# Attention scores by row-tiled matmuls instead of zero-padded queries, in an encoder layer on eight cores

## Chip, cores and metric

One Trainium2 chip, all eight NeuronCores; each core works on one of eight sequences with no traffic between cores. The time is that of the slowest core, in device microseconds (us). Executions come in a fast state and sometimes in a slow one, in which cores of one die run longer at a lower granted clock (one execution of the kernel before, in the set of `tile_oldconst`, took 947.07 us: 937.7 to 945.5 us on one die at a mean clock of 0.826 to 0.831, 806.7 to 813.3 on the other at 0.989 to 0.993; in the fast runs of all kernels no core's mean is under 0.978); only fast runs are compared. PE is the tensor engine (PEld its weight loads), ACT the scalar engine, DVE the vector engine. PSUM (`ps` in the records) is the memory into which the matmuls here write, which the planner hands out in banks; copying a result out of it, by ACT or DVE (`kT<-ps`: 0.69 and 0.75 us before), is called an eviction. The MLP is the second half of the layer, with `w_up` and `w_down`.

## The reference, cut to what matters

```python
h = modulate(rms_norm(x, g_mix), sh1, sc1)            # (2048, 1024) a sequence
proj = h @ w_in                                       # [fourier 512 | q 512 | k 512 | v 512]
y_f  = rms_norm(fourier_mix(u_f, w_four), g_four_out)
y_na = rms_norm(neighbourhood_attention(q, k, v, rpb), g_na_out)   # 8 heads of 64, window 8 rows x 16 columns
x = x + gt1 * (concat([y_f, y_na]) @ w_out)
h2 = modulate(rms_norm(x, g_ffn), sh2, sc2)
up = dwconv_centred(h2 @ w_up, conv_w, conv_b)        # width 3
x = x + gt2 * ((silu(up[..., :2816]) * up[..., 2816:]) @ w_down)
return rms_norm(x, g_final)
```

## The kernel before

A kernel is built as a list of operations with their tiles. A planner written in the kernel's own Python places them on the engines before launch: at each step it takes, over all engines, the operation that can start earliest, with durations from small formulas (the "planning constants"), and so fixes each engine's order and the PSUM banks. (Conditioning weights, below, are the matrix `w_ada` that makes the shifts and scales `sh`, `sc` and `gt`.) Change a duration or an operation, and every engine's order can change.

Attention handles 16 query tiles of 128 queries. Two heads of 64 features share a tile of 128 partitions. To keep them apart, queries are stored block-diagonally (`qbd`): for each head a copy in which the other head's 64 rows are zero. Each projection of queries is therefore evicted from PSUM twice, with a 0/0.125 mask as scale. A "unit" is one head pair of one query tile (64 units): four matmuls against four blocks of 128 keys, each with 256 columns (two heads x 128 queries), into two banks; inner tiles have an extra block ("extra scores").

```python
# query eviction, twice: e = 0, 1
for e in range(2):
    EVAC(qbd[:, 4*tb:4*tb+4, j-4, e, :], <PSUM>, 512, ..., scale=hm[:, e:e+1], bias=bqe[:, j-4, e:e+1], tag="q_ev")
# ... cut ...
bs = Bank(2, SB_)                                     # SB_ = banks 0-1 or 2-3
mms([(bs, None)], [(V(bs, c//2, (c%2)*256, (c%2+1)*256), kT[:, hp, (jb+c)*128:(jb+c+1)*128],
                    qbd[:, i, hp, :, :], True, True) for c in range(4)], "qk")
ACT(pf, <both banks>, AF.Exp, 1024, ...)              # then x exp(bias) on DVE, then the value product
# ... cut: planning constants ...
def act_ns(n, psum, ptr=0, accum=False): return n / 1.2 + 110 + 85 * ptr + (200 if accum else 0)
def dve_ns(n, mode=1.0):                 return n / (0.96 * mode) + 130
DMA_RATE = 290.0; DMA_LAT = 1900.0
```

The rest of the mixer stage (input projection, Fourier transform, output projection, second norm) is planned into the same stretch of time as attention; the MLP comes after it.

The softmax here doesn't subtract the row's maximum and nothing guards it: scores larger than these inputs give would overflow.

## Time and profile before

| | before |
|---|---|
| median of the first three runs | 814.93 us (814.04 to 815.93) |
| spans of the cores, profiled run | 804.1 to 814.7 us |
| mixer stretch: first projection matmul to first matmul of the MLP | 282.7 us mean of eight cores, 279.5 us on core 4 |
| matmuls of the MLP and after (core 4) | 323.2 to 796.3 us, not touched by the change |

Lines of the page of the slowest core (core 1): its span, the busy time of each engine with its share, and the chain of work that ended last, by engine.

```profile
span 814.7 us, 11668 instructions; the slowest of 8 cores (804.1 to 814.7 us)
...
PE 750.1 (92%) x4781; PEld 381.3 (47%) x4781; DVE 553.7 (68%) x752; ACT 449.8 (55%) x695; POOL 50.0 (6%) x91
...
PE 76%; DMA 11%; ACT 7%; DVE 4%; issue 1%; SPq 0%; POOL 0%; POOLq 0%
```

The chain is mostly PE; but most of that is the MLP.

The table of windows of core 4: for each window busy us of the engines (instructions), granted PE clock, DMA share, GB/s.

```profile
core 4: us, PE busy (x) PEld busy (x) DVE busy (x) ACT busy (x) POOL busy (x), PEclk, DMA share, GB/s
...
140.00:200.00 60.00, 55.08 (x593) 33.79 (x592) 43.54 (x86) 46.64 (x82) 3.70 (x7) 1.00 0.76 185
...
260.00:300.00 40.00, 38.47 (x348) 23.09 (x347) 32.99 (x73) 38.75 (x93) 2.14 (x4) 1.00 0.73 208
...
sum 305.00, PE 287.78 PEld 166.59 DVE 211.47 ACT 254.34 POOL 17.70; mean PE 47.96 PEld 27.77 DVE 35.24 ACT 42.39 POOL 2.95
```

From 140 to 200 us and from 260 to 300 us nothing is idle for long: PE 92% to 96%, ACT 78% to 97%, DVE 73% to 82%, DMA about three quarters.

What touches the query tile on core 4: count, shortest/median/longest in ns, first and last start in us.

```profile
L694 PE MATMUL ps<-qbd,kT x304: 219/272/283, 63.7 to 286.1; 128*128 128x256 bf16 x128, 128*128 128x128 bf16 x24
L761 ACT ACTIVATE qbd<-ps,bqe,colp_s x19: 761/777/801, 62.9 to 216.4; 128x512 bf16<-128x512 f32 x19
L766 DVE TENSOR_SCALAR qbd<-ps,colp_s,bqe x13: 800/807/811, 61.8 to 175.7; 128x512 bf16<-128x512 f32 x13
```

304 score matmuls (256 of them 256 columns wide; the counts after the semicolon, here x128 and x24, are of a sample, here every second matmul) and 32 evictions, 19 x 0.777 + 13 x 0.807 = 25 us of ACT and DVE.

The timeline of PE around one unit (start, us, what):

```profile
121.42 0.60 PE L694 MATMUL ps<-qbd,kT 128*128 128x256 bf16 x4
121.86 0.29 PE L694 MATMUL ps<-Vx,pT_80 128*128 128x65 bf16 x4
```

The four score matmuls start at 121.42 and the next group at 121.86: 0.44 us a unit.

The first starts of the input projection and of the MLP's up projection on core 4 (two views of tiles, one line each; after the shortest, median and longest duration stand the first and the last start):

```profile
L694 PE MATMUL ps<-hT_64,win x192: 376/379/634, 43.7 to 192.4; 128*128 128x512 bf16 x192
```

### The profile page before, as it was taken

The numbers are of one execution on the slowest core, as the hardware profiler recorded it, in microseconds if no ns is written. First come the engines' busy times: TensorE is split into PE (matmuls) and PEld (weight loads), VectorE is DVE, ScalarE is ACT, GpSimd is POOL, SyncE is SP. The second block draws the span as 40 slices with busy tenths as digits, with TensorE's granted clock in tenths as the row PEclk, the third lists the DMA queues.
The fourth block names the chain that finished last, engine by engine and source line by source line (L and its number), as shares of the span: only waits on it lengthen the run. The fifth ranks groups of instructions, "written<-read, shape, count | busy, mean of one in ns | idle before, by whom it ended". The sixth has DMA issues, their size and how long they took to land.

```text
span 814.7 us, 11668 instructions; the slowest of 8 cores (804.1 to 814.7 us)
## 1 busy us (share of the span) xinstructions
PE 750.1 (92%) x4781; PEld 381.3 (47%) x4781; DVE 553.7 (68%) x752; ACT 449.8 (55%) x695; POOL 50.0 (6%) x91
## 2 busy tenths in 40 slices
PE   1269999889999899989999999999999999999996
PEld 1134566456465555544444444444444454444442
DVE  2348596468577785459898989898988954443343
ACT  4468897678679898764545454545454503111112
POOL 0000000010000000122000000000000110000000
PEclk9999999989999999999999999999999999999999
DMA  8899763995311559999222222222223472232321
GB/s 229 292 293 304 231 125 69 189 185 166 100 54 35 185 137 286 238 161 162 39 39 40 38 36 35 37 40 38 39 39 40 40 142 104 103 130 104 125 83 77
DMA packets 38613, 97.87 MB, mean 120 GB/s; under 512 B 11808, under 2 KB 12192, under 8 KB 37536
## 3 DMA queue, kind: packets, MB, share of 16 engines
q1 hardware_dynamic: 18864, 71.30, 26.4%
q0 software_dynamic: 19696, 25.83, 22.8%
q8 instruction: 37, 0.61, 0.3%
q14 instruction: 16, 0.13, 0.1%
HBM read 106.16 MB, written 16.78 MB: 151 GB/s over the span
## 4 chain that ended last, share of the span: by engine, by line
PE 76%; DMA 11%; ACT 7%; DVE 4%; issue 1%; SPq 0%; POOL 0%; POOLq 0%
PE ps L694 75%; DMA mst_100<-w_ada 2%; DMA mst_98<-w_ada 1%; PE ps L699 1%; DMA mst_99<-w_ada 1%; DMA xs_129<-x 1%; DMA stb_127<-w_ada 1%; DMA stb_125<-w_ada 1%; DMA stb_128<-w_ada 1%; DMA xr_135<-x 1%; DMA stg_122<-w_in 1%; ACT pT_80 L719 1%; ACT pT_81 L719 1%; DMA xs_131<-w_out 1%; ACT pT_79 L719 1%
## 5 line engine op out<-in xcount | busy, mean ns | idle before, releaser
L694 PE MATMUL ps<-wd,aT 128*128 128x512 bf16 x704 | 152.4, 379 | 0.0
L731 DVE SCALAR_TENSOR_TENSOR accv<-ps,colp_s,accv 128x1023 f32<-128x1023 f32 (+1 forms) x88 | 112.6, 1280 | 33.4 <-ACT accv L719 32.5
L731 DVE SCALAR_TENSOR_TENSOR accg<-ps,colp_s,accg 128x1023 f32<-128x1023 f32 (+1 forms) x88 | 112.7, 1280 | 7.9 <-ACT accg L719 6.4
L694 PEld LDWEIGHTS ps<-wd,aT 128*128 128x128 bf16 x704 | 68.7, 98 | 82.4
L719 ACT ACTIVATE accg<-ps,colp_s 128x1024 f32<-128x1024 f32 x44 | 53.0, 1206 | 96.4 <-PE ps L694 96.4
L719 ACT ACTIVATE sgm<-accg 128x1024 bf16<-128x1024 f32 x44 | 46.5, 1057 | 44.5 <-DVE accg L731 44.4
L694 PE MATMUL ps<-hT_61,wup_86 128*128 128x512 bf16 x256 | 56.9, 379 | 1.9 <-ACT hT_61 L761 1.9
L719 ACT ACTIVATE accv<-ps,colp_s 128x1024 f32<-128x1024 f32 x44 | 52.6, 1195 | 9.1 <-PE ps L694 9.1
L694 PE MATMUL ps<-hT_61,wup_87 128*128 128x512 bf16 x256 | 56.6, 379 | 0.0
L725 DVE TENSOR_TENSOR aT<-sgm,accv 128x1024 bf16<-128x1024 bf16 x44 | 53.5, 1216 | 0.0
L694 PE MATMUL ps<-hT_64,win 128*128 128x512 bf16 x192 | 48.6, 401 | 2.0 <-DVE win L725 2.0
L694 PE MATMUL ps<-hT_61,wup_89 128*128 128x512 bf16 x224 | 49.5, 379 | 0.0
L694 PE MATMUL ps<-hT_61,wup_91 128*128 128x512 bf16 x224 | 49.5, 379 | 0.0
L694 PE MATMUL ps<-hT_61,wup_88 128*128 128x512 bf16 x224 | 49.5, 379 | 0.0
L694 PE MATMUL ps<-hT_61,wup_90 128*128 128x512 bf16 x224 | 49.5, 379 | 0.0
L694 PE MATMUL ps<-hT_65,win 128*128 128x512 bf16 x192 | 43.9, 379 | 0.0
L725 DVE TENSOR_TENSOR td_153<-ps,gt_140 128x512 f32<-128x512 f32 x16 | 11.1, 691 | 45.6 <-PE ps L694 45.6
L694 PE MATMUL ps<-qbd,kT 128*128 128x256 bf16 (+1 forms) x304 | 41.3, 274 | 0.5 <-ACT pT_80 L719 0.3
L694 PEld LDWEIGHTS ps<-hT_61,wup_86 128*128 128x128 bf16 x256 | 24.9, 98 | 31.8 <-ACT hT_61 L761 2.1
L694 PEld LDWEIGHTS ps<-hT_61,wup_87 128*128 128x128 bf16 x256 | 25.0, 98 | 30.2
L694 PE MATMUL ps<-wo,yna 128*128 128x512 bf16 x128 | 33.5, 384 | 1.6 <-DVE yfT L763 0.8
L694 PEld LDWEIGHTS ps<-hT_61,wup_88 128*128 128x128 bf16 x224 | 21.9, 98 | 26.4
(364 smaller groups left out, 1141.7 us busy)
## 6 DMA issues: line engine op xcount, KB each, us to landing
wd<-w_down POOLq DMA_DIRECT2D x22, 256.0 KB, 6.2
xs_129<-x SPq DMA_DIRECT2D x6, 512.0 KB, 7.3
mst_98<-w_ada SPq DMA_DIRECT2D x3, 1024.0 KB, 7.2
mst_99<-w_ada SPq DMA_DIRECT2D x3, 1024.0 KB, 6.9
xs_130<-x SPq DMA_DIRECT2D x5, 512.0 KB, 6.7
xs_131<-x SPq DMA_DIRECT2D x5, 512.0 KB, 6.9
mst_100<-w_ada SPq DMA_DIRECT2D x2, 1024.0 KB, 6.7
stg_121<-w_in SPq DMA_DIRECT2D x4, 512.0 KB, 5.7
```

The source lines that it names most:

```text
L694: return [e.matmul(of(), lhsT=l, rhs=r, start=s0, stop=s1) for of, l, r, s0, s1 in items]
L699: return [e.transpose(out=of(), in_=i, identity=ident) for of, i in items]
L719: return P.add("act", lambda e: e.activation(out=out, in_=(in_() if callable(in_) else in_), func=func, **kw), act_ns(n, callable(in_), pt ...
L725: return P.add(eng, lambda e: e.tensor_tensor(out=out, in0=in0() if callable(in0) else in0, in1=in1() if callable(in1) else in1, op=op), d ...
L731: return P.add("dve", lambda e: e.scalar_tensor_tensor(out=out, in0=in0() if callable(in0) else in0, scalar=s, in1=in1() if callable(in1) ...
```

## The change

Intent: store queries once (`qT`, scaled by 0.125), and let two 64-row matmuls, one a head, run side by side in the upper and lower half of the array, each into its own bank. That removes the multiplications by zero and half of the query evictions. The planner gets a duration of 320 ns for the eight matmuls of a unit (it had counted 437 ns for four), new formulas, meant to be more exact, for ACT and DVE, other DMA constants, and the conditioning weights get a fourth staging buffer. The diff, cut to its core:

```diff
-DMA_RATE = 290.0
-DMA_LAT = 1900.0
+DMA_RATE = 270.0
+DMA_LAT = 2300.0
-    return n / 1.2 + 110 + 85 * ptr + (200 if accum else 0)
+    return n / 1.2 + (50 if psum else 93) + 93 * ptr + (93 if accum else 0)
-def dve_ns(n, mode=1.0):
-    return n / (0.96 * mode) + 130
+def dve_ns(n, mode=1.0, ptr=0):
+    return n / (0.96 * mode) + 65 + 61 * ptr
 ... (callers pass ptr; tables and tiles re-laid out; masks removed) ...
-        mst = [... for i, o_ in enumerate((R3, R3 + 8 * K, R2))]
+        mst = [... for i, o_ in enumerate((R3, R3 + 8 * K, Q0 + 32 * K, Q0 + 40 * K))]
-                for e in range(2):
-                    EVAC(qbd[:, 4 * tb:4 * tb + 4, j - 4, e, :], ..., scale=hm[:, e:e + 1], bias=bqe[:, j - 4, e:e + 1], tag="q_ev")
+                EVAC(qT[:, 4 * tb:4 * tb + 4, j - 4, :], ..., scale=0.125, bias=bc_, tag="q_ev")
-                bx = Bank(1, FB_)          # extra scores: 4 matmuls of 128 columns, one exponential of 512
+                bx = Bank(2, [4, 5, 6])    # 8 matmuls of 64 rows x 64 columns, two exponentials of 256, dur=280.0
-                    mms([(bs, None)], [(... V(bs_, c // 2, (c % 2) * 256, (c % 2 + 1) * 256)), kT[:, hp, ...],
-                                        qbd[:, i, hp, :, :], True, True) for c in range(4)], "qk")
+                    mms([(bs, None)], [(... V(bs, e, c * 128, (c + 1) * 128)), kT[e * 64:(e + 1) * 64, hp, ...],
+                                        qT[e * 64:(e + 1) * 64, i, hp, :], True, True)
+                                       for c in range(4) for e in range(2)], "qk", dur=320.0)
```

More of the change, by code (lines that the diff above doesn't have):

```diff
@@ L478, in _layout_inputs @@
     g = np.where(valid[None], g, f32(-1e30))
-    ua = g[:, :16].reshape(4, 2, 8, 2, 128, 64).transpose(4, 0, 2, 1, 3, 5).reshape(128, 4 * 8 * 2 * 2 * 64)
-    ux = g[:, 17].transpose(1, 0, 2).reshape(128, 512)
+    ua = g[:, :16].reshape(4, 2, 8, 2, 128, 64).transpose(4, 0, 1, 2, 3, 5).reshape(128, 4 * 8 * 2 * 2 * 64)
+    ux = g[:, 17].reshape(4, 2, 128, 64).transpose(2, 1, 0, 3).reshape(128, 512)
     utab = np.zeros((9, 128, 1024), f32)
@@ L496, in _layout_inputs @@
            np.asarray(inp["conv_w"][0], f32).reshape(3, 44, 128).transpose(2, 0, 1).reshape(128, 132),
-           col(inp["conv_b"][0], 44), 0.125 * (np.arange(128)[:, None] // 64 == np.arange(2)[None, :]).astype(f32)], axis=1)
+           col(inp["conv_b"][0], 44)], axis=1)
     shared = dict(_CONST)
@@ L539, in build_nc @@
     w_down = din("w_down", [DFF, D])
-    colp_d = din("colp", [128, 234])
+    colp_d = din("colp", [128, 232])
     utab_d = din("utab", [9, 128, 1024])
@@ L571, in build_nc @@
         ctab = small("ctab_s", [128, 514], BF16)
-        colp = small("colp_s", [128, 234], F32)
+        colp = small("colp_s", [128, 232], F32)
         ccs = small("ccs", [128, 8], F32)
@@ L581, in build_nc @@
         bcol = small("bcol", [128, 12], F32)
-        bqe = small("bqe", [128, 4, 2], F32)
         ss = small("ss", [128, 5, 16], F32)
@@ L599, in build_nc @@
         cb = colp[:, 188:232]
-        hm = colp[:, 232:234]
         R0 = 3200
@@ L616, in build_nc @@
         R2 = R1 + 16 * K
-        pT = [T(f"pT{i}", R2 + i * 2 * K, [128, 4, 2, 2, 64], BF16) for i in range(3)]
-        pX = [T(f"pX{i}", R2 + 6 * K + i * 2 * K, [128, 4, 2, 2, 64], BF16) for i in range(2)]
+        pT = [T(f"pT{i}", R2 + i * 2 * K, [128, 2, 4, 128], BF16) for i in range(3)]
+        pX = [T(f"pX{i}", R2 + 6 * K + i * 2 * K, [128, 2, 4, 2, 64], BF16) for i in range(2)]
         peX = [T(f"peX{i}", R2 + 10 * K + i * K, [128, 512], BF16) for i in range(2)]
@@ L625, in build_nc @@
         R3 = R2 + 16 * K
-        U = T("U", R3, [128, 4, 8, 256], BF16)
+        U = T("U", R3, [128, 4, 2, 8, 128], BF16)
         UX = T("UX", R3 + 16 * K, [128, 512], BF16)
-        mst = [T(f"mst{i}", o_, [128, 8, 256], F32) for i, o_ in enumerate((R3, R3 + 8 * K, R2))]
         Q0 = R3 + 17 * K
-        qbd = T("qbd", Q0, [128, NT, 4, 2, 128], BF16)
-        yna = T("yna", Q0, [128, NT, 8, 128], BF16)
+        mst = [T(f"mst{i}", o_, [128, 8, 256], F32) for i, o_ in enumerate((R3, R3 + 8 * K, Q0 + 32 * K, Q0 + 40 * K))]
+        qT = T("qT", Q0, [128, NT, 4, 128], BF16)
+        yna = T("yna", Q0, [128, NT, 4, 128], BF16)
         kT = T("kT", Q0 + 32 * K, [128, 4, S], BF16)
@@ L732, in STT @@
                                                                  in1=in1() if callable(in1) else in1, op0=op0, op1=op1),
-                         dve_ns(n), reads=rd, writes=[out], banks=banks, tag=tag)
+                         dve_ns(n, 1.0, 0 if isinstance(s, float) else 1), reads=rd, writes=[out], banks=banks, tag=tag)
         def TS(out, in0, s1, op0, n, mode=1.0, s2=None, op1=None, banks=(), tag="ts"):
@@ L742, in fn @@
                 return e.tensor_scalar(out=out, in0=in0() if callable(in0) else in0, **kw)
-            return P.add("dve", fn, dve_ns(n, mode), reads=rd, writes=[out], banks=banks, tag=tag)
+            return P.add("dve", fn, dve_ns(n, mode, sum(not isinstance(v, float) for v in (s1, s2) if v is not None)), reads=rd, writes=[out],
+                         banks=banks, tag=tag)
         def EVAC(out, in_, n, banks, mode=1.0, scale=None, bias=None, tag="evac", engs=("act", "dve")):
@@ L766, in fn @@
                 return e.tensor_scalar(out=out, in0=src, scalar1=scale, scalar2=bias, op0=ALU.mult, op1=ALU.add)
-            op = P.add(engs, fn, {"act": act_ns(n, True, ptr), "dve": dve_ns(n, mode)}, reads=rd, writes=[out], banks=banks, tag=tag)
+            op = P.add(engs, fn, {"act": act_ns(n, True, ptr), "dve": dve_ns(n, mode, ptr)}, reads=rd, writes=[out], banks=banks, tag=tag)
             return op
@@ L785, in fn @@
                 return e.tensor_scalar(out=out, in0=in_, scalar1=r_, scalar2=None, op0=ALU.mult)
-            op = P.add(("dve", "act"), fn, {"act": act_ns(n, False, 1), "dve": dve_ns(n, 2.0) + 80}, reads=[in_, r_], writes=[out], tag=tag)
+            op = P.add(("dve", "act"), fn, {"act": act_ns(n, False, 1), "dve": dve_ns(n, 2.0, 1)}, reads=[in_, r_], writes=[out], tag=tag)
             return op
@@ L799, in build_nc @@
         load("sp", ctab, ctab_d, "c1", 131072)
-        load("sp", colp, colp_d, "c2", 119808)
+        load("sp", colp, colp_d, "c2", 118784)
         MEMSET("dve", epsb, EPS, 1)
@@ L839, in mod_load32 @@
             nmw[0] += 1
-            st_ = mst[n % 3]
+            st_ = mst[n % 4]
             k = next_stg()
-            load("sp", st_, w_ada[blk, q], f"mst{n % 3}", 1048576, tag="wada")
+            load("sp", st_, w_ada[blk, q], f"mst{n % 4}", 1048576, tag="wada")
             CP("act", stb[k][:, 0:4, :], st_[:, 0:4, :], 1024, tag="wada_cast")
@@ L910, in bias_col @@
             mms([(b, None)], [((lambda: V(b, 0, 0, 1)), r3[:, kc, :], sh1[:, kc:kc + 1], kc == 0, kc == 7) for kc in range(8)], "bias")
-            if 4 <= j < 8:
-                TS(bqe[:, j - 4, :], hm, lambda: V(b, 0, 0, 1), ALU.mult, 2, banks=[(b, None)], tag="bias_fin")
-            else:
-                CP("dve", bcol[:, j:j + 1], lambda: V(b, 0, 0, 1), 1, banks=[(b, None)], tag="bias_fin")
+            TS(bcol[:, j:j + 1], lambda: V(b, 0, 0, 1), 0.125 if 4 <= j < 8 else 1.0, ALU.mult, 1, banks=[(b, None)], tag="bias_fin")
         def fm_group(tb, j):
@@ L930, in fm_evac @@
             elif j < 8:
-                for e in range(2):
-                    EVAC(qbd[:, 4 * tb:4 * tb + 4, j - 4, e, :], lambda: V(b, 0, 0, 512).rearrange("p (t q) -> p t q", t=4), 512,
-                         [(b, None)], scale=hm[:, e:e + 1], bias=bqe[:, j - 4, e:e + 1], tag="q_ev")
+                EVAC(qT[:, 4 * tb:4 * tb + 4, j - 4, :], lambda: V(b, 0, 0, 512).rearrange("p (t q) -> p t q", t=4), 512,
+                     [(b, None)], scale=0.125, bias=bc_, tag="q_ev")
             else:
@@ L976, in build_nc @@
                 load("sp", stg[k], utab_d[k9], f"stg{k}", 524288, tag="utab")
-                ACT(U[:, k9 // 2, 4 * (k9 % 2):4 * (k9 % 2) + 4, :].rearrange("p m n -> p (m n)"), stg[k], AF.Exp, 1024, tag="utab_exp")
+                ACT(U[:, k9 // 2, k9 % 2, :, :].rearrange("p m n -> p (m n)"), stg[k], AF.Exp, 1024, tag="utab_exp")
             else:
@@ L996, in attn_tile @@
             if inner:
-                bx = Bank(1, FB_)
+                bx = Bank(2, [4, 5, 6])
                 px = pX[i % 2]
                 pex = peX[i % 2]
-                mms([(bx, None)], [((lambda hp=hp: V(bx, 0, hp * 128, (hp + 1) * 128)), kT[:, hp, (jb + 4) * 128:(jb + 5) * 128],
-                                    qbd[:, i, hp, :, 64:128], True, True) for hp in range(4)], "qkx")
-                ACT(pex, lambda: V(bx, 0, 0, 512), AF.Exp, 512, banks=[(bx, None)], tag="expx")
-                TT("dve", px.rearrange("p h e a q -> p (h e) a q")[:, :, 1, :], pex.rearrange("p (g q) -> p g q", g=8),
+                mms([(bx, None)],
+                    [((lambda hp=hp, e=e: V(bx, e, hp * 64, (hp + 1) * 64)), kT[e * 64:(e + 1) * 64, hp, (jb + 4) * 128:(jb + 5) * 128],
+                      qT[e * 64:(e + 1) * 64, i, hp, 64:128], True, True) for hp in range(4) for e in range(2)], "qkx", dur=280.0)
+                for e in range(2):
+                    ACT(pex[:, e * 256:(e + 1) * 256], lambda e=e: V(bx, e, 0, 256), AF.Exp, 256, banks=[(bx, e)], tag="expx")
+                TT("dve", px.rearrange("p e h a q -> p (e h) a q")[:, :, 1, :], pex.rearrange("p (g q) -> p g q", g=8),
                    UX.rearrange("p (g q) -> p g q", g=8), ALU.mult, 512, mode=2.0, tag="mulx")
@@ L1011, in attn_tile @@
                     bs = Bank(2, SB_)
-                    mms([(bs, None)], [((lambda c=c: V(bs_, c // 2, (c % 2) * 256, (c % 2 + 1) * 256)), kT[:, hp, (jb + c) * 128:(jb + c + 1) * 128],
-                                        qbd[:, i, hp, :, :], True, True) for bs_ in (bs,) for c in range(4)], "qk")
-                    pf = pt.rearrange("p c e a q -> p (c e a q)")
+                    mms([(bs, None)], [((lambda c=c, e=e, bs=bs: V(bs, e, c * 128, (c + 1) * 128)),
+                                        kT[e * 64:(e + 1) * 64, hp, (jb + c) * 128:(jb + c + 1) * 128], qT[e * 64:(e + 1) * 64, i, hp, :], True, True)
+                                       for c in range(4) for e in range(2)], "qk", dur=320.0)
+                    pf = pt.rearrange("p e c n -> p (e c n)")
                     ACT(pf, (lambda bs=bs: ps[:, bs.phys:bs.phys + 2, :].rearrange("p b n -> p (b n)")), AF.Exp, 1024,
@@ L1027, in attn_tile @@
                     for c0, c1, sl in parts:
-                        w = pf[:, c0 * 256:c1 * 256]
-                        TT("dve", w, w, U[:, hp, sl:sl + c1 - c0, :].rearrange("p m n -> p (m n)"), ALU.mult, (c1 - c0) * 256, mode=2.0,
+                        w = pt[:, :, c0:c1, :].rearrange("p e c n -> p e (c n)")
+                        TT("dve", w, w, U[:, hp, :, sl:sl + c1 - c0, :].rearrange("p e m n -> p e (m n)"), ALU.mult, (c1 - c0) * 256, mode=2.0,
                            tag="mul")
@@ L1035, in attn_tile @@
                         for c in range(4):
-                            items.append((of, pt[:, c, e, :, :], Vx[:, jb + c, h, :], c == 0, c == 3 and not inner))
+                            items.append((of, pt[:, e, c, :], Vx[:, jb + c, h, :], c == 0, c == 3 and not inner))
                         if inner:
-                            items.append((of, px[:, hp, e, :, :], Vx[:, jb + 4, h, :], False, True))
+                            items.append((of, px[:, e, hp, :, :], Vx[:, jb + 4, h, :], False, True))
                     mms([(bo, None)], items, "pv")
@@ L1052, in attn_tile @@
             trs([(bt, None)], [((lambda c=c: Vb(bt)[:, c * 128:(c + 1) * 128]), ob[:, c * 128:(c + 1) * 128]) for c in range(4)], "tro")
-            EVAC(yna[:, i, 0:4, :].rearrange("p c t -> p (c t)"), lambda: Vb(bt)[:, 0:512], 512, [(bt, None)], mode=2.0, tag="yna_ev")
+            EVAC(yna[:, i, :, :].rearrange("p c t -> p (c t)"), lambda: Vb(bt)[:, 0:512], 512, [(bt, None)], mode=2.0, tag="yna_ev")
         def inproj(tb, part):
```

## The prediction

> **What bounds the kernel now.** The chain of waits puts 76% on the tensor engine (PE), 11% on DMA, 7% on ACT, 4% on DVE. From about 353 us on (gated MLP, down projection) the chain is one unbroken run of matmuls, 454 us long, which the change does not touch. The change can act only on the first 353 us. There the table of windows shows three regimes: 0 to about 65 us, DMA (share 0.85 to 1.0 in most windows, PE nearly idle); 65 to 297 us, where attention, input projection, Fourier and output projection are interleaved, with PE busy about 95%, ACT about 80%, DVE about 70%; and 297 to 353 us, output projection and second norm. The chain in the middle stage is mostly PE, with ACT stretches at 92-112, 246-256 and 288-296 us, and DMA (conditioning weights) at 135-175 us.
>
> **What changes, costed.**
> 1. Score matmuls. Before: 64 units of 4 matmuls with 256 columns, half of them multiplied by zeros. In the timeline eight start within 0.87 us, 109 ns each, so 435 ns a unit, 28 us in all; the extra-block scores take 48 x 56 ns = 2.7 us. After: 8 matmuls of 64 rows and 128 columns a unit. If two run side by side at the 56 ns at which 128-column transposes start here, a unit would take 224 ns; but every matmul also needs its own weight load, and the closest pace shown is 31 ns for a matmul with its load (value products, 65 columns), so at least about 250 ns. The diff plans 320 ns (and 280 ns for the extra block, against 4 x 56). [...] Saving: 64 x 115 ns = 7.4 us, minus 12 x 57 ns = 0.7 us: 6.7 us of PE.
> 2. Query evictions: 32 (19 on ACT at 0.78 us, 13 on DVE at 0.81 us: 25 us) become 16 with one pointer less, about 0.7 us: 14 us less over two engines, before 225 us.
> 3. The extra exponential splits in two: [...] it also takes two adjacent banks of a pool of four.
> 4. A fourth staging buffer in the DMA-bound opening: 1 to 2 us at most, because the bytes remain.
> 5. New planning constants: every engine's order is replanned. Gain or loss of some us, not computable from the trace.
>
> **On the critical path.** Of item 1 some 70-80% (PE is the limit of most of the middle stage, but also waits on ACT and DMA there): 5 us. Of item 2 the part in ACT-bound stretches: 2 to 3 us. Item 4: 1 us. Item 5: 1 us gain expected, uncertain by 4. Sum about -9.5 us: 805.5 us, range 797 to 812.
>
> **What would show it.** Score matmuls: 512 + 96 in place of 304, a unit starting within about 0.32 us (right) or over 0.43 us (wrong); query evictions x16; MLP run again about 454 us long, starting at 341 to 347 us instead of 353; ACT stretches near 92-112 us shorter; first input-projection matmul 0 to 2 us earlier than 45.5 us.
>
> **What would make it wrong.** [...] a stage that turns out bound by ACT exponentials (64 x 0.91 us) or by conditioning-weight DMA, so that PE savings become idle time; the replanned order moving transfers into each other; a better plan than I credit, gaining over 16 us.

The sum is 5 (item 1) + 2.5 (item 2) + 1 (item 4) + 1 (item 5) = 9.5 us; the 320 ns of item 1 are the diff's plan. The 70-80% of item 1, the 2 to 3 us of item 2, item 4 and item 5 are estimates of mine, with no measured number behind them. What the trace of before shows for the rest: as many weight loads as matmuls on PE (4781 each); starts 56 ns apart for 128 columns and 29 to 30 ns for the value products (the record has 31); evictions with one pointer less, those of `kT`, at 0.69 us on ACT and 0.75 on DVE; exponentials of 1024 columns at 1.02 us whole, of which 0.91 us stands in the chain.

## More of the kernel before

```profile
L694 PE MATMUL ps<-hT_61,wup_86 x256: 379/379/389, 323.2 to 633.9; 128*128 128x512 bf16 x128
```

323.2 - 43.7 = 279.5 us of mixer stretch.

## The result, and the profile after

812.5 us median of four runs (811.68 to 813.85) against 815.43 us of before's four, one of them slow. The ratio of fast runs is 0.9971, with a 95% interval of 0.9949 to 0.9993: about 2.4 us faster, where I had said 9.5, and just above the range of 797 to 812 us. (Ratios here are the mean time of one kernel's fast runs over the mean of the other's fast runs of the same rounds, so they are not quite ratios of the medians quoted.) Run again on another chip it gave 0.9977.

The page of the slowest core after (core 6):

```profile
span 810.9 us, 12199 instructions; the slowest of 8 cores (803.2 to 810.9 us)
...
PE 736.2 (91%) x4999; PEld 369.6 (46%) x5085; DVE 549.5 (68%) x746; ACT 447.4 (55%) x697; POOL 49.2 (6%) x91
...
PE 75%; ACT 12%; DMA 8%; DVE 2%; issue 1%; SPq 0%; POOLq 0%
```

ACT's share of the chain has risen from 7% to 12%, while the PE share is as before. The MLP hides how large this is. Within the mixer stretch alone, as a mean of the eight cores, PE held 53% of the chain before (ACT 22%, DMA 15%, DVE 8%) and 53% after (ACT 35%, DMA 6%, DVE 4%). On the slowest cores, ACT's part of the chain between 255 and 300 us grew from 10.5 to 34.6 us. The windows of core 4 after:

```profile
core 4: us, PE busy (x) PEld busy (x) DVE busy (x) ACT busy (x) POOL busy (x), PEclk, DMA share, GB/s
...
140.00:200.00 60.00, 56.52 (x706) 33.66 (x705) 40.69 (x83) 48.34 (x87) 4.14 (x8) 1.00 0.77 179
...
260.00:300.00 40.00, 36.78 (x374) 20.53 (x369) 30.17 (x68) 39.08 (x89) 2.88 (x6) 1.00 0.80 230
...
sum 305.00, PE 282.84 PEld 156.05 DVE 204.99 ACT 251.22 POOL 16.66; mean PE 47.14 PEld 26.01 DVE 34.16 ACT 41.87 POOL 2.78
```

In the sum line PE's busy time fell by 5 us, ACT's by 3 and DVE's by 6.5; in the window from 260 to 300 us ACT is busy 98% and PE 92% (before: 97% and 96%).

The query tile after, on core 4:

```profile
L692 PE MATMUL ps<-qT,kT x608: 189/216/227, 67.8 to 284.5; 64*128 64x128 bf16 x128, 64*128 64x64 bf16 x24
L765 DVE TENSOR_SCALAR qT<-ps,bcol x9: 745/751/752, 65.5 to 166.6; 128x512 bf16<-128x512 f32 x9
L760 ACT ACTIVATE qT<-ps,bcol x7: 672/687/687, 68.0 to 216.3; 128x512 bf16<-128x512 f32 x7
```

608 score matmuls of 64 rows and 16 evictions of 0.69 or 0.75 us: as planned, 11.6 us in place of 25.

The timeline of PE on core 4 after:

```profile
108.06 0.62 PE L692 MATMUL ps<-qT,kT 64*128 64x128 bf16 x16
108.61 1.90 PE L692 MATMUL ps<-winv,hT_64 128*128 128x512 bf16 x8
...
111.26 0.29 PE L692 MATMUL ps<-Vx,pT_80 128*128 128x65 bf16 x4
111.38 0.20 PE L692 MATMUL ps<-Vx,pX_81 128*128 128x65 bf16 x1
111.51 0.40 PE L692 MATMUL ps<-qT,kT 64*128 64x128 bf16 x8
111.84 0.39 PE L692 MATMUL ps<-winv,hT_64 128*128 128x512 bf16 x1
```

Read three things. Two units in a row (16 matmuls) take 108.61 - 108.06 = 0.55 us. One unit alone takes 111.84 - 111.51 = 0.33 us until the next full-array matmul starts. And the last value product ahead of it starts at 111.38; the next matmul could have started 29 ns later, at 111.41, but the tiled one starts at 111.51. From the single records over the whole trace: the two halves of a pair start 3 to 4 ns apart, the next pair 53 ns later, so four pairs stream in 226 ns; but going from full-array to tiled costs 96 ns over the usual distance (for instance 312 in place of 216 ns after a 512-column matmul), and going back costs 95 ns (148 in place of 53). Each such step, in or out, is called a switch below; here it costs about 95 ns. What happens in the array during it the trace does not show.

So a unit alone costs 226 + 191 = 417 ns, hardly less than the 436 ns of before (436 / 226 = 1.9 without the switches, 436 / 417 = 1.05 with them); two in a row cost 321 ns each, which is the 320 ns of the plan. Of the 51 groups in which the plan issued tiled matmuls, 31 hold only eight. Adding up all score matmuls: 30.6 us before; 15.8 us of streaming plus 102 switches for 9.7 us after. PE work fell by 5.1 us.

The trace of before already held a delay of this size, and I overlooked it when I made the prediction. There, two groups of matmuls have weights with a single column (`128*1`). On every core the step into them takes 309 or 310 ns where 216 is usual, and the step out 152 in place of 56 or 312 in place of 216, so 93 to 96 ns each way. That these delays have the same cause as the switches was not tested. The first group, on core 4 of before:

```profile
216.72 0.59 PE L694 MATMUL ps<-winv,hT_65 128*128 128x512 bf16 x2
217.24 0.38 PE L694 MATMUL ps<-AB,ue_58 128*1 128x128 bf16 x4
217.56 0.34 PE L694 MATMUL ps<-AB,uT 128*128 128x128 bf16 x3
```

The ends of the stretch on core 4 after:

```profile
L692 PE MATMUL ps<-hT_63,win x192: 376/379/634, 46.9 to 194.3; 128*128 128x512 bf16 x192
```

```profile
L692 PE MATMUL ps<-hT_60,wup_85 x256: 379/379/390, 326.7 to 637.3; 128*128 128x512 bf16 x128
```

326.7 - 46.9 = 279.8 us, against 279.5 before, on two cores whose clock never dropped in it. Taking for every core the usual distance between starts for the form of each matmul (216 ns for 512 columns, 109 for 256, 56 for 128, 29 for 65, 25 for one), and calling the rest pauses, I get for core 4 (a half-clock spell is a time in which the granted clock is 0.50, and what it costs counts as pause too): before 254.1 us of work and 25.4 of pauses, after 239.3 + 9.7 us of work and 30.8 of pauses. The 5 us of PE work came back as 5 us of pauses. Over all eight cores the stretch is 282.7 us before, 281.0 after.

On undisturbed cores nothing was gained (280.1 us before, mean of three; 279.9 after, mean of four); the 1.7 us over all cores come with fewer spells of half clock. On core 1 before, PE waited for conditioning weights:

```profile
174.67 0.59 PE L694 MATMUL ps<-cs,stb_127 128*128 128x1 bf16 x16 [2.96 <-DMA stb_127<-w_ada]
```

and the windows of core 1 around it show what followed (columns as above):

```profile
170.00:173.80 3.80, 1.56 (x25) 0.96 (x21) 3.00 (x7) 2.60 (x3) 0.00 (x0) 1.00 1.00 199
173.80:180.60 6.80, 5.93 (x68) 4.72 (x69) 2.74 (x8) 3.72 (x7) 1.06 (x2) 0.50 0.90 196
```

PE was 41% busy for 3.8 us, and then the granted clock was 0.50 for 6.8 us. The 15 spells in the stretch (before and after together) last 3.4 us, two of them 6.8. In the 3.4 us before this one PE was busy for a third of the time, with no pause over 2.2 us, and in the 3.4 us before each of the 15 it was busy for 26 to 64%, with no pause over 2.3 us. What brings a spell on is not shown beyond that. Before, five of the eight cores had such a spell in the stretch, up to 10.2 us a core; after, four had, up to 6.8 us. On core 1 the pause was a wait for a transfer (2.96 us, above); how many cores have spells varies from run to run (five had one when the changed kernel ran again).

What happened to ACT's share of the saved evictions: over the whole program ACT's instructions sum to 491.3 us on before's slowest core and 487.4 us on after's, 4 us less, though query evictions fell there by 10.0 us. The splitting of the extra exponential took 1.9 us (24 x 0.384 in place of 12 x 0.609), and the new plan put 5 more of the wide norm scalings (1.15 us on ACT, 0.75 on DVE) and 3 more transposed-input evictions (1.02 against 0.69) on ACT, and fewer of other evictions.

### The profile page after: what moved, and what is told of

Its sections match the earlier page's. It is cut to its first block, busy times and chain, and to the rows that moved or that the text cites. A ratio compares the mean times of both kernels' runs of the same rounds, so it can differ in the third digit from the quotient of the medians.

```text
span 810.9 us, 12199 instructions; the slowest of 8 cores (803.2 to 810.9 us)
## 1 busy us (share of the span) xinstructions
PE 736.2 (91%) x4999; PEld 369.6 (46%) x5085; DVE 549.5 (68%) x746; ACT 447.4 (55%) x697; POOL 49.2 (6%) x91
## 4 chain that ended last, share of the span: by engine, by line
PE 75%; ACT 12%; DMA 8%; DVE 2%; issue 1%; SPq 0%; POOLq 0%
PE ps L692 74%; DMA xs_130<-x 2%; ACT pT_80 L717 1%; ACT rstd L717 1%; DMA stb_127<-w_ada 1%; ACT pT_79 L717 1%; ACT pT_78 L717 1%; DMA wf<-w_four 1%; DMA mst_97<-w_ada 1%; DMA mst_100<-w_ada 1%; PE ps L697 1%; DMA mst_99<-w_ada 1%; DMA stg_121<-w_in 1%; DMA mst_98<-w_ada 1%; ACT hT_60 L760 1%
## 5 line engine op out<-in xcount | busy, mean ns | idle before, releaser
L692 PE MATMUL ps<-hT_63,win 128*128 128x512 bf16 x180 | 44.5, 389 | 9.0 <-DVE sh_51 L723 3.7
L692 PE MATMUL ps<-hT_64,win 128*128 128x512 bf16 x184 | 42.7, 379 | 0.8 <-issue 0.6
L723 DVE TENSOR_TENSOR td_153<-ps,gt_140 128x512 f32<-128x512 f32 x16 | 11.1, 691 | 44.9 <-PE ps L692 44.9
L692 PEld LDWEIGHTS ps<-hT_60,wup_85 128*128 128x128 bf16 x256 | 24.9, 98 | 31.7 <-ACT hT_60 L760 2.0
L692 PEld LDWEIGHTS ps<-hT_60,wup_86 128*128 128x128 bf16 x256 | 25.1, 98 | 30.2
L692 PEld LDWEIGHTS ps<-hT_60,wup_90 128*128 128x128 bf16 x224 | 21.9, 98 | 26.4
L692 PEld LDWEIGHTS ps<-hT_60,wup_88 128*128 128x128 bf16 x224 | 21.9, 98 | 26.4
L692 PEld LDWEIGHTS ps<-hT_60,wup_87 128*128 128x128 bf16 x224 | 21.9, 98 | 26.4
```

The source lines that it names most:

```text
L692: return [e.matmul(of(), lhsT=l, rhs=r, start=s0, stop=s1) for of, l, r, s0, s1 in items]
L723: return P.add(eng, lambda e: e.tensor_tensor(out=out, in0=in0() if callable(in0) else in0, in1=in1() if callable(in1) else in1, op=op), d ...
```

## The experiments

Two theories at the start. **A**: the stretch is bound by PE, tiling did save 5 us, and an unlucky new order gave them back. **B**: PE had stopped being what decides there; other engines and transfers decide, so less PE work turns into pauses. All ratios are to the kernel before in the same rounds, five rounds each; the changed kernel stands at 0.9971 and 0.9977. I give differences to the changed kernel as differences of these ratios times 815 us. The runs were made in four sets of four, each set on one chip: `tile_oldconst`, `pad_newconst`, `score_twice`, `more_switches`; `after_again`, `u_half`, `q_ev_twice`, `pair_units`; `act_light`, `both_light`, `norm_on_dve`, `pair_norm_dve`; and the last four below. Only the second set has the changed kernel itself beside it, so differences in the other sets go through before, on another chip. Each ratio has a 95% interval of about +-0.002 to 0.003, so a difference of two of them is uncertain by 2 to 3 us, and a worth of PE time below by about 0.2 (`pair_switches`: 0.4).

**1. Which part of the change?** `tile_oldconst`: the changed kernel with before's planning constants.

```diff
-    return n / 1.2 + (50 if psum else 93) + 93 * ptr + (93 if accum else 0)
+    return n / 1.2 + 110 + 85 * ptr + (200 if accum else 0)
# likewise dve_ns, DMA_RATE, DMA_LAT
```

> The changed kernel planned with the planning constants of before (tiled matmuls, single query eviction, four staging buffers kept). Theory A (the tiling saves about 5 us of PE after its switches, and the new plan gives it back as waits): 3 to 6 us faster than the changed kernel, about 806 to 809 us, ratio to before 0.990 to 0.994. Rival B (the middle stage is bound by ACT, DVE and DMA, so less PE work turns into idle time under any plan): as the changed kernel, 811 to 814 us.

Measured: 817.15 us median, ratio 0.9986 (0.9964 to 1.0008). Theory A's 0.990 to 0.994 fails here: with the old constants the tiled kernel is not shown to be faster than before. PE work is 239.6 + 11.2 us (59 groups), pauses 33.5 us.

`pad_newconst`: the kernel before with the new constants.

> The kernel before (padded queries, two evictions) with only the planning constants changed. Theory A: the new constants cost 3 to 6 us, so 818 to 821 us, and PE slack between the first projection matmul and the first up matmul grows by about 5 us. Rival B: the constants alone do nothing, 813 to 817 us.

Measured: 818.68 us, ratio 1.0027 (1.0004 to 1.0049), about 2 us slower. On its four undisturbed cores the stretch is 285.4 us where before's three have 280.1: as theory A had it and theory B did not, though the slowest core shows only half of that. (Before's slowest core spent 10.2 us of the stretch at half clock; in this kernel's profile one core had one half-clock spell, of 3.4 us.) The two together make a square (ratios; padded/old is 1):

| | old constants | new constants |
|---|---|---|
| padded, two evictions | 1 | 1.0027 |
| tiled, one eviction | 0.9986 | 0.9971, 0.9977 |

The same tiling (with the single eviction) is worth 1 us under one plan and 4 under the other, and the constants cost 2 us on the padded kernel and gain 1 on the tiled one. Apart from the 4 us none of these is well clear of its uncertainty, so this square suggests, and does not show, that the parts do not add; `pair_oldconst` below shows it.

**2. What is PE time worth there?** The order on every engine stays fixed in these runs; only instructions within an operation change, and the planner is not told. `score_twice` issues every pair twice.

```diff
+  its = [it for k in range(0, len(items), 2) for it in items[k:k + 2] * 2] if tag == "qk" else items
```

> The changed kernel, same order on every engine, every pair of score matmuls issued twice (same result): 64 x 226 ns = 14.5 us more PE work in tiled mode, no switch more. Theory A (PE bound there): 10 to 14.5 us slower than the changed kernel, 822 to 827 us. Rival B: the waits absorb most, under 6 us slower.

Measured: 819.14 us, ratio 1.0028 (1.0009 to 1.0047): about 4.4 us slower for 14.1 us more PE work, so 0.3 us for each. Pauses fell to 25.3 us. Theory B.

`more_switches` puts one full-array column in the middle of each unit.

```diff
+  mid=(V(bs, 1, 384, 385), kT[:, hp, jb*128:(jb+1)*128], qT[:, i, hp, 0:1], True, True)
+  its = items if mid is None else items[:4] + [mid] + items[4:]
```

> The changed kernel, same order, one full-array matmul of one column in the middle of each of the 64 units (its column is overwritten afterwards, same result): two more mode switches a unit. If a switch costs 95 ns each way as the trace of the change suggests, 64 x (2 x 95 + 25) = 13.8 us more PE time; theory A: 9 to 14 us slower than the changed kernel. If the 95 ns were an artefact of the records (waits on banks or on data), each unit would grow by 25 to 60 ns only and the time by under 4 us.

Measured: 821.85 us, ratio 1.0057 (1.0027 to 1.0086), about 6.8 us slower for 13.1 us more, so 0.5 for each. The cost of a switch is confirmed in the timeline. The same two units with the extra scores, on core 6 of the changed kernel:

```profile
101.44 0.74 PE L692 MATMUL ps<-qT,kT 64*128 64x128 bf16 x24
102.11 1.90 PE L692 MATMUL ps<-winv,hT_64 128*128 128x512 bf16 x7
```

and on core 3 of this one:

```profile
102.30 1.17 PE L693 MATMUL ps<-qT,kT 64*128 64x128 bf16 x26
103.40 0.82 PE L693 MATMUL ps<-winv,hT 128*128 128x512 bf16 x3
```

102.11 - 101.44 = 0.67 us against 103.40 - 102.30 = 1.10 us: 0.43 us for two inserted columns, 215 ns each, of which a single column without switches takes 25 ns (from start to start in the traces of before and after). The 60 ns in the expectation was an estimate of mine.

`u_half` is the opposite: it leaves out half of the contraction of the Fourier channels' projection (wrong result).

```diff
+  its = items[:3] + items[7:] if tag == "u_half" else items
```

`after_again` is the changed kernel as control on that chip.

> The changed kernel itself, as control on this chip for the three others. Ratio to before 0.995 to 0.999.

> The changed kernel, same order, with 4 of the 8 contraction chunks of the Fourier channels' projection left out (wrong result on purpose): 64 x 216 ns = 13.8 us less PE work, all of it within the middle stage, nothing else touched. Theory A (the stage is PE-bound and the 5 us saved by tiling were lost to an unlucky order): 8 to 13 us faster than the changed kernel, about 800 to 805 us. Rival B (PE has stopped being the limit there, other engines and transfers decide): under 4 us faster, PE slack in the stretch grows by about 10 us or more.

Measured: 0.9977 (0.9958 to 0.9995) for the control, 0.9935 (0.9905 to 0.9964) for `u_half`: 3.4 us faster for 13.8 us less PE work, so a quarter of it. (The two intervals touch, and one of the six fast executions, 814.88 us, lies 6 us above the next; without it the gain would be 4.6 us, a third.) The first starts of the two projections on core 1, control first, neither core with a half-clock spell:

```profile
L692 PE MATMUL ps<-hT,win x384: 376/379/634, 46.7 to 217.0; 128*128 128x512 bf16 x192
```

```profile
L692 PE MATMUL ps<-hT,wup x1408: 379/379/390, 327.8 to 645.3; 128*128 128x512 bf16 x176
```

```profile
L693 PE MATMUL ps<-hT,win x320: 376/379/631, 44.9 to 210.3; 128*128 128x512 bf16 x160
```

```profile
L693 PE MATMUL ps<-hT,wup x1408: 379/379/390, 321.2 to 638.6; 128*128 128x512 bf16 x176
```

327.8 - 46.7 = 281.1 and 321.2 - 44.9 = 276.3 us. PE work fell from 249.2 to 235.4 us and pauses grew from 32.8 to 43.1 us (means of the cores with complete records). This run and `score_twice` decide for B as to what PE time is worth: most of the PE work taken away or added went into pauses or came out of them.

Half-clock spells blur these numbers: the profile of `score_twice` has none in the stretch, that of the control has at least one on five cores. On the cores without any drop of the clock in it, the stretch is 279.9 us in both profiles of the changed kernel, 287.3 in `score_twice` (four cores), 286.2 in `more_switches` (two) and 277.1 in `u_half` (two): 0.5 for each microsecond added and 0.2 for each taken away. All of this is the worth in the order of the changed kernel; in the order of before it was not measured.

**3. What decides instead?** `q_ev_twice` makes each query eviction twice, first into an unused region, which undoes that part of the change.

```diff
+  return [one(e, also), one(e, out)] if also is not None else one(e, out)   # also = unused tile
```

> The changed kernel, same order, every query eviction made twice (first into an unused region), so the evictions that the change removed are back: 7 x 0.69 us on ACT and 9 x 0.75 us on DVE, 11.5 us of engine time. If the removal was worth the 2 to 3 us that I predicted: 2 to 3 us slower than the changed kernel. If ACT and DVE bound the stage: up to 6 us slower. If the removal was worth nothing (spread over idle time): within 1 us.

Measured: 815.78 us, ratio 1.0011 (0.9989 to 1.0034): 2.8 us slower than the control. By the middle of its interval, which overlaps the control's, the single eviction is worth what I predicted, 2 to 3 us. (The run puts back 11.5 us of the 14.)

`act_light` takes the sums of squares of the four norms before the MLP over 64 columns (wrong result).

```diff
+  k_ = 64 if tag in ("sq1", "sq2", "sqf", "sqo") else None     # out[:, :k_], in_[:, :k_], scale (n / k_) ** 0.5
```

> The changed kernel, same order, with the sums of squares of all four norms taken over 64 columns and scaled (wrong result on purpose): 32 x 0.80 us + 32 x 0.37 us = 37 us less ACT work before the MLP, of 303 us, PE work untouched. If ACT bounds the middle stage: 8 us or more faster than the changed kernel (ratio to before under 0.989). If neither ACT nor PE alone does and the pauses are dependency chains that hand over between them: 2 to 6 us faster. If ACT is off the path: under 1 us.

Measured: 808.07 us, ratio 0.9921 (0.9903 to 0.9939): about 4.3 us faster for 37 us less ACT work (an estimate: in the trace of the changed kernel these squares take 1.06 us for 1024 columns and 0.63 for 512, so 0.84 ns a column). So ACT alone doesn't bound the stretch either.

`both_light` does both.

> act_light and u_half together (wrong result on purpose), same order: 13.8 us less PE and 37 us less ACT. u_half alone gave 3 us. If PE and ACT hold each other (each is the next limit when the other is relieved), the sum is clearly more than the two gains added: 10 us or more faster than the changed kernel. If DMA or DVE is the limit behind both, it stays near the two gains added, 4 to 8 us.

Measured: 803.63 us, ratio 0.9863 (0.9846 to 0.9879): about 9 us faster, little more than 3.4 + 4.3. With 14 us less PE and 37 us less ACT there are still 36.5 us of pauses in 272 us. What stands behind the two (DVE, transfers, or the length of the dependency chains in a fixed order) these runs do not tell apart; I leave it open. The inferred chain only shows that no one engine takes over: within the stretch (mean of eight cores) it is PE 59%, DVE 17%, ACT 12%, DMA 8% in `act_light` and PE 51%, DVE 19%, ACT 16%, DMA 10% in `both_light`.

`norm_on_dve` tested the suspicion that ACT lost its relief to the operations that the new plan moved to it.

```diff
-  op = P.add(("dve", "act"), fn, ...)            # norm scaling
+  op = P.add("dve" if n == D else ("dve", "act"), fn, ...)
# and engs=("dve",) for the transposed-input eviction
```

> The changed kernel with the 32 wide norm scalings and 16 transposed-input evictions pinned to DVE (ACT takes 1.15 and 1.02 us for what DVE does in 0.75 and 0.69 us; the new plan had moved 9 of them from DVE to ACT): about 36 us less on ACT, 24 us more on DVE before the MLP. If the evictions that the plan moved to ACT ate the gain of the single query eviction: 2 to 5 us faster than the changed kernel. If DVE is as near its limit: within 1 us or slower.

Measured: 813.32 us, ratio 0.9978 (0.9958 to 0.9998): no difference. The suspicion is not confirmed; but the pinning also makes a new plan (53 groups in place of 51), which could hide a gain, so it is not refuted either.

**4. Fewer switches.** `pair_units` issues two units as one block over banks 0 to 3, the extra scores with the first, so 32 groups in place of 51.

```diff
-  bs = Bank(2, SB_); mms([(bs, None)], <8 matmuls of one unit>, "qk", dur=320.0)
+  bp = Bank(4, [0]); mms(xbanks + [(bp, None)], xitems + <16 matmuls of two units>, "qk", dur=640.0 + 15.0 * len(xitems))
```

> The changed kernel with the two units of a half (and the extra block) issued as one block of tiled matmuls over four banks: 32 groups in place of 51, so 38 switches less, 38 x 95 ns = 3.6 us of PE. The order changes. Theory A: 2 to 4 us faster than the changed kernel. Rival B: within 1.5 us, or slower because a pair holds four banks until two exponentials are done.

Measured: 810.57 us, ratio 0.9944 (0.9919 to 0.9968), correct: 2.7 us faster than the control on the same chip (whose interval it overlaps) and the fastest correct kernel, about 4.6 us under before. By count, switches cost 6.1 us in place of 9.7 (64 and 102, at about 95 ns).

`pair_norm_dve` adds the pinning of `norm_on_dve`.

> The paired version with the same pinning. If the two add: 4 to 7 us faster than the changed kernel, ratio to before about 0.990. If the paired order already covers the ACT waits: as the paired version, ratio 0.994.

Measured: 814.99 us, ratio 1.0000 (0.9984 to 1.0017): the gain of pairing is gone, pauses 38.6 us. Neither expectation was right; the plan that the pinning makes here is worse.

The cause of the constants' cost and of pairing's gain were open. Four more:

`pair_switches` inserts a full-array column between the two units of a block, in the same order.

```diff
+  its = items if mid is None else items[:-8] + [mid] + items[-8:]
```

> The paired version, same order, with one full-array matmul of one column between the two units of each pair (overwritten afterwards, same result): 64 switches back, 32 x (190 + 25) ns = 6.9 us of PE. If the paired version gains by saved switches: 2 to 4 us slower than the paired version (ratio to before 0.997 to 0.999). If it gains by its order: under 1 us slower (ratio below 0.996).

Measured: 813.85 us, ratio 0.9982 (0.9964 to 1.0000): 3.1 us slower than the paired version (on another chip; the intervals touch) for 6.7 us more PE time. In this order a PE microsecond is worth about 0.45, so the saved switches of pairing (3.6 us) account for about 1.7 of its 2.7 us; the rest is its order, or noise.

`pad_engconst` and `pad_dmaconst` split the new constants on the padded kernel.

```diff
# pad_engconst: new act_ns, dve_ns; old DMA_RATE, DMA_LAT.   pad_dmaconst: the reverse
```

> The kernel before with the new durations of ACT and DVE in the plan, the old two DMA constants. If the engine durations reorder the plan for the worse: the stretch from the first projection matmul to the first up matmul is 284 to 286 us on undisturbed cores as with all new constants (280 with the old ones), ratio 1.002 to 1.006. If the DMA constants do it: 279 to 281 us, ratio 0.999 to 1.001.

> The kernel before with the new two DMA constants in the plan, the old engine durations. The opposite of pad_engconst: 284 to 286 us if the DMA constants do it, 279 to 281 us if not. If both stay at 280 us, it is the combination, and the plan is simply sensitive.

Measured: 822.76 us, ratio 1.0091 (1.0067 to 1.0114) with the engine durations alone; 815.99 us, ratio 1.0006 (0.9990 to 1.0022) with the DMA constants alone (every core had a half-clock spell in the stretch, so the expected 279 to 281 us can't be checked). The engine durations reorder for the worse, by more than I expected (stretch 289.3 us on the one undisturbed core), and the new DMA constants take most of it back when both are new (1.0027).

`pair_oldconst` plans the paired version with the old constants.

> The paired version planned with the constants of before. If the new constants cost about 2 us in every version: ratio to before 0.991 to 0.993, the fastest correct kernel of the study. If their cost is peculiar to one plan: within 1.5 us of the paired version (0.9944) either way.

Measured: 827.23 us, ratio 1.0134 (1.0111 to 1.0158), against 0.9944 with the new ones: 15 us, the other way round from what I expected. All eight cores had several half-clock spells between 297 and 360 us, and mean pauses were about 46 us. So the new constants cost 2 us in one structure, gain 1 in another and 15 in a third: what a set of constants is worth is a property of the one plan that it produces.

## Why the prediction was wrong

- **What bounds the kernel.** Wrong in the one phrase on which the rest leans, "PE is the limit of most of the middle stage". The numbers that I read (PE about 95%, ACT about 80%, DVE about 70%) were right, but a busy share counts recorded durations that overlap (379 ns against 216 from start to start); by start-to-start times PE had 254 us of work in 280. Even that, 91%, does not make it the limit: PE held 53% of the chain within the stretch, and `u_half` shows that 13.8 us less PE work moves the time by 3.4 us.
- **Item 1, size.** "The diff plans 320 ns", which the saving takes over: true for two units in a row (321 ns), not for one alone (417 ns), and 31 of 51 groups were of eight matmuls. The saving was 5.1 us, not 6.7. Two thirds of the gain went into switches, at about 95 ns each: of 14.8 us of saved streaming, 9.7 went into 102 of them.
- **The step that failed: "Of item 1 some 70-80% ... 5 us".** The prediction itself named the danger, "so that PE savings become idle time", but gave it no weight in the sum. Measured with the order fixed, a microsecond of PE work is worth 0.25 (`u_half`), 0.3 (`score_twice`) to 0.5 (`more_switches`) us. 5.1 us times that is 1.3 to 2.6 us, an estimate from these runs. The rest became pauses. (On core 4 the pauses grew by 5.4 us, as much as the work shrank, but there the new constants have a share in it.)
- **Item 2.** Held: 14 us less eviction time, 2.8 us measured by `q_ev_twice` (0.5 to 5 with its uncertainty), though of the 10 us taken from ACT the new plan gave 6 back.
- **Item 4.** Nothing: the first projection matmul starts at 45.0 us before and 44.9 us after (means of eight cores). I had said 0 to 2 us earlier and counted 1. That the buffer itself did nothing is argued from this, not tested alone.
- **Item 5, "1 us gain expected, uncertain by 4".** On the padded kernel this is a second step that failed. The new constants alone made the padded kernel about 2 us slower (5.3 us in the stretch of undisturbed cores), and the engine durations alone 7 us; on the tiled kernel they gained 1 us, within noise. By the square, of the 7 us by which the prediction was off, 4 lie in items 1, 2 and 4 and 3 in item 5 if the constants are counted first, and all of it in items 1, 2 and 4 if they are counted last. Durations meant to be more exact did not give a better plan.
- **Signs.** 608 score matmuls and 16 evictions: right. A unit within about 0.32 us: half right, see above. ACT stretches near 92-112 us shorter: hardly (between 85 and 120 us ACT holds 19.1 us of the slowest core's chain before and 18.1 after), and ACT stretches came in from 255 to 300 us. The MLP and what follows unchanged: right (473.1 us on core 4 before, 473.0 after). The MLP 6 to 12 us earlier: wrong, its first matmul starts at 327.7 us before and at 325.9 after (means of eight cores).
- **As a check**, an estimate that adds the measured pieces: -1.3 to -2.6 (item 1), -2.8 (item 2), +2.2 (constants on the padded kernel) gives -1.9 to -3.2 us; measured were -1.9 and -2.4. These pieces don't strictly add, so the agreement is no proof. The cores without a drop of the clock give a harsher balance: there the constants cost 5.3 us (280.1 to 285.4, on two chips), the rest of the change gained 5.5 (285.4 to 279.9), and nothing was left. So the 2.4 us that the slowest cores gained may be largely luck with half-clock spells, five cores before and four after; that the gain came again on another chip (0.9977) with five such cores in its profile speaks against luck alone, and it stays open.

## What to carry to other kernels

Here row tiling paid by group, not by matmul: count how often the order steps between full-array and tiled matmuls, and put enough tiled work between two steps (here 191 ns for going in and out, against 210 ns saved by one unit). Where PE, ACT, DVE and DMA are all three quarters full, ask what a microsecond on the engine is worth before multiplying it out: add or remove some work within a fixed order and see; here it was 0.25 to 0.5 us with PE 92% to 94% busy from 140 to 200 and 260 to 300 us. And where an automatic planner fixes the order, a change of its cost formulas is a second change, here up to 15 us large, and should be measured apart from the first.
